# Second MLP: half of block 0's first product by seven products of quarters, temporaries and tables in pools of their stages

## The chip, the cores and the metric

One core of a Trainium2 chip runs the program in one launch. The metric is the device time of one execution in microseconds (us), the median of several runs. One core has five engines that run side by side, each through a queue of its own in order: TensorE (PE, matrix products; the loads of its stationary operand are shown apart as PEld), VectorE (DVE), ScalarE (ACT), GpSimd (POOL) and SyncE (SP, which here only issues DMA transfers).

## The reference, cut to what matters

Two layers work on 640 tokens (512 latent, 128 context) of width 1024. Layer 0 mixes tokens by pooling, layer 1 by retention, and each is followed by the MLP in question:

```python
def sq_relu_mlp(h, w1, w2):
    return jnp.square(jax.nn.relu(h @ w1)) @ w2

# per layer i, with shift, scale and gate from the conditioning vector
h = rmsnorm(x, norm_mlp_w[i]) * (1 + sc_m) + sh_m
x = x + g_m * sq_relu_mlp(h, mlp_w1[i], mlp_w2[i])      # w1 1024 x 4096, w2 4096 x 1024
```

The change lies in the MLP of layer 1 (the second MLP) and in where temporaries and small tables are kept.

## The kernel before

**Layout and precision.** Activations are held transposed: 8 tiles of 128 channels by 640 tokens, and the tokens go in two halves of 320 (`HALVES`). Every operand of a product is split into a high and a low part (`split`, L142: ScalarE casts the high part at L144, VectorE subtracts the low one at L145), and one product of tiles is three matmuls (`mm3`, L205 to L207). A plain product of one 128-column tile of the weights with one half of the tokens (`gemm`, L209) is 8 x 3 = 24 matmuls of 320 columns.

**The MLP.** `mlp` (L748 on) goes through four blocks of 1024 hidden channels. In each block the first product fills `act` (8 tiles n, two halves h): ScalarE's relu (L851) and square (L852), then a split. The second product adds to x (`add_to_x`, L500). Block 0 makes its first product plainly: `follow` (L530) makes tiles 0 to 3 while the norm of the second half of the tokens is still being computed, then tiles 4 to 7 come one by one. Blocks 1 to 3 (`FAST`) make theirs in two halves of four tiles, each by seven products of quarters in place of eight (`fast`, L812).

**Seven products of quarters.** `seven` (L790) loads two pieces of the weights (1 MB each), makes four sums of 128x1024 on VectorE (L802 to L806) and seven split operands. `quarters` (L767) makes the operands of the other side from the eight normed tiles `hm`: for each of four q it joins four high and low parts (L776), makes four sums (L777, L779, L781, L783) and splits them, three of them into a tile `both` of their own, shown as `tq` in the trace, and one over `hm[q]`'s second half in place. That is 12 operations of VectorE and 4 casts of ScalarE for each q, once for the MLP, ahead of block 1. Of the seven products, the first two read `hm[0..3]` and `hm[4..7]` of the first half as they are, the third and fourth read `tq`, the fifth what was written in place, the sixth `hm[4..7]` of the second half, the seventh `tq`. Each is 24 matmuls, with q as the inner index: of a product's two tiles of output, each takes q = 0, 1, 2, 3 in turn.

**What sets the order.** The Tile framework puts the program's instructions into the engines' queues ahead of time and places semaphores; the queues of the kernel before are not in the order of the text. For instance, the operations of `quarters` stand in the text behind block 0's whole second product, and in VectorE's queue among its `add_to_x`. Buffers are handed out per pool and tag: staged weights from `wst` (2 buffers), split weights from `wsp` (tags whi, wlo, 4 buffers each), temporaries by `th` and `t5` from `tmp` (tag t, 7 buffers of 128x512, for all stages of the kernel).

**Tables.** Retention's rotation table is the rear part of `tab_sb`, loaded at L644 on SP's queue near the start; its position tables `npos` and `ipos` (GpSimd, L734 to L737) and the constant `ones_v` (L232) are made when the engines come to them, and all stay in the pool `const` for the whole kernel.

Of the kernel before, what the change touches and what calls it, by code (L numbers as in the profile page):

```python
# [27 lines left out]
DV = 512  # L28
# [35 lines left out]

STEPS = (((0, 0, 0, 0, 3, 2, 3, 0), (0, 1, 0, 1, 0, 0, 0, 0)),
# [45 lines left out]
def hybrid_kernel(ctx: ExitStack, tc: tile.TileContext, x_prompt, x_sample, state_ret, c, c_ctx, w_ada, b_ada,  # L111
# [15 lines left out]
    tmp = ctx.enter_context(tc.tile_pool(name="tmp", bufs=1))  # L127
    psum = ctx.enter_context(tc.tile_pool(name="psum", bufs=8, space=PSUM))


    def bank():
        return psum.tile([128, 512], F32, tag="ps", name=nm("ps"))

# [4 lines left out]
    def t5():  # L138

        return tmp.tile([128, 512], F32, tag="t", name=nm("t"), bufs=7)  # L140
# [68 lines left out]
    def gemm(ws, act, h, mid=None):  # L209


        out = [bank()[:, 0:HALF] for _ in ws]
        for k in range(len(act)):
            if mid and k == len(act) // 2:
                mid()
            for o, w in zip(out, ws):
                mm3(o, [z[:, k] for z in w], [z[:, HALVES[h]] for z in act[k]], k == 0, k == len(act) - 1)
        return out
# [199 lines left out]
    xall = xp.tile([128, KD, TOK], F32, name="xall")  # L418
# [132 lines left out]
    with tc.tile_pool(name="pool", bufs=1) as pp:  # L551
        extra[:] = [(wst, 2), (pp, 3), (pp, 3), (wst, 2), (pp, 3)]
# [153 lines left out]
    def decays():  # L706
# [38 lines left out]
        tables.extend((lg, nlg, npos, ipos, zeta))  # L745
# [3 lines left out]
    def mlp(i, sq, norm, hm, step, along):  # L749

        with tc.tile_pool(name=f"hid{i}", bufs=1) as hid:

# [92 lines left out]

            for b in range(4):
                act = [[hid.tile([128, TOK], F32R, tag=f"a{n}{e}", name=nm("a")) for e in "hl"] for n in range(8)]

                def hidden(n, h, ps):
                    r, f = th(), th()  # L850
                    S.activation(r, ps, AF.Relu)  # L851
                    S.activation(f, r, AF.Square)  # L852
                    split(f, *[z[:, HALVES[h]] for z in act[n]])
# [9 lines left out]
                if b in FAST[i]:  # L863
                    if b == FAST[i][0]:
                        ops = quarters()
                    for half in range(2):
                        fast(b, half, ops, hidden)
                        if i == 0 and b == 3:
                            next(logs, None)
                            next(logs, None)  # L870
                    get(2 * b + 1, 0)
                else:
                    for n in range(4 if b == 0 else 0, 8):
                        if n == FREE:
                            room[0] = room[1]
                        for h in range(2):
                            hidden(n, h, gemm([get(2 * b, n)], hm, h)[0])
                        step(STEPS[b][0][n])
                if i == 0 and b == 0:
                    step(until=(0, 5))  # L880
                if b == 3:
                    room[:] = [None, None]
                    return tail(lambda n, h: gemm([get(7, n)], act, h)[0], mod[i][5], along)
                for n in range(KD):
# [22 lines left out]
    with tc.tile_pool(name="ret", bufs=1) as rp:  # L907
        def r5():
            return rp.tile([128, 512], F32R, tag="r5", name=nm("r5"), bufs=6)

        lg, nlg, npos, ipos, zeta = tables
# [5 lines left out]
        def queries_keys(hd):  # L917
# [10 lines left out]
            def take(nmq, t, h, ps):  # L928
                ct = C_ROPE if nmq == "q" else C_ROPE + 144
# [11 lines left out]
                if t == 0:  # L941
                    cb, sb = (tab_sb[:, ct + o:ct + o + 8][:, rw].unsqueeze(2).to_broadcast(shape) for o in (0, 8))
                else:
                    cb, sb = (tab_sb[:, ct + o:ct + o + 64].unsqueeze(1).to_broadcast(shape) for o in (16, 80))
# [301 lines left out]
```

## Time and profile before

| | |
|---|---|
| time, median of 3 runs | 1621.87 us (1620.45 to 1624.13) |
| the profiled execution's own time | 1622.77 us |
| its span, first to last instruction | 1621.0 us |
| mean granted clock of TensorE, share of full speed | 0.994 |
| matmuls | 9897 |

A row of a timeline gives the start from the span's begin, the duration, the engine, the line of the kernel, the operation, the tiles as output <- inputs, sizes, and in brackets the idle time of the engine before it and what ended that. Matmuls are pipelined: the distance of two starts is the pace, not the duration shown.

### The profile page before, as it was taken

The numbers are of one execution on the slowest core, as the hardware profiler recorded it, in microseconds if no ns is written. First come the engines' busy times: TensorE is split into PE (matmuls) and PEld (weight loads), VectorE is DVE, ScalarE is ACT, GpSimd is POOL, SyncE is SP. The second block draws the span as 40 slices with busy tenths as digits, with TensorE's granted clock in tenths as the row PEclk, the third lists the DMA queues.
The fourth block names the chain that finished last, engine by engine and source line by source line (L and its number), as shares of the span: only waits on it lengthen the run. The fifth ranks groups of instructions, "written<-read, shape, count | busy, mean of one in ns | idle before, by whom it ended". The sixth has DMA issues, their size and how long they took to land. (4 is left out here: it accounts for less than half of the span.)

```text
span 1621.0 us, 24493 instructions
## 1 busy us (share of the span) xinstructions
PE 1582.8 (98%) x9897; PEld 1473.6 (91%) x9897; DVE 1164.0 (72%) x2254; ACT 727.0 (45%) x1338; POOL 11.7 (1%) x26
## 2 busy tenths in 40 slices
PE   6999999999999999999999999999999999999997
PEld 3459999999999988889889988998899999999997
DVE  6879996676766687886797678778967573554654
ACT  6747326336156354433442443353464371451640
POOL 0000000000000000000000000000000000000000
PEclk9999999999999999999999999999999999999999
DMA  9744333333314123323304241322032132131221
GB/s 356 252 141 146 105 105 104 104 124 111 105 53 156 45 70 128 96 79 130 128 29 156 63 146 64 118 92 91 26 105 79 34 124 78 53 104 53 95 75 66
DMA packets 137954, 169.83 MB, mean 105 GB/s; under 512 B 3512, under 2 KB 111472, under 8 KB 137840
## 3 DMA queue, kind: packets, MB, share of 16 engines
q1 hardware_dynamic: 134800, 161.28, 30.2%
q0 software_dynamic: 1312, 4.20, 0.8%
q10 hardware_dynamic: 1728, 2.78, 0.5%
q8 instruction: 78, 1.28, 0.3%
q14 instruction: 36, 0.29, 0.1%
HBM read 161.43 MB, written 6.82 MB: 104 GB/s over the span
## 5 line engine op out<-in xcount | busy, mean ns | idle before, releaser
L144 ACT CAST whi<-wst 128x1024 fp32r<-128x1024 f32 x245 | 254.4, 1049 | 422.5 <-PE ps L206 200.8
L145 DVE TENSOR_TENSOR wlo<-wst,whi 128x1024 fp32r<-128x1024 f32 x245 | 297.3, 1223 | 136.5 <-ACT whi L144 124.0
L205 PE MATMUL ps<-a,whi 128*128 128x320 f32 x896 | 277.2, 310 | 1.2 <-ACT a L144 1.2
L206 PE MATMUL ps<-a,whi 128*128 128x320 f32 x896 | 277.3, 310 | 0.1
L207 PE MATMUL ps<-a,wlo 128*128 128x320 f32 x896 | 276.2, 309 | 0.0
L500 DVE SCALAR_TENSOR_TENSOR xall<-ps,mod,xall 128x320 f32<-128x320 f32 (+2 forms) x288 | 115.7, 436 | 151.6 <-PE ps L207 150.4
L206 PEld LDWEIGHTS ps<-a,whi 128*128 128x128 f32 x896 | 168.2, 188 | 2.1 <-DVE a L145 1.7
L205 PEld LDWEIGHTS ps<-a,whi 128*128 128x128 f32 x896 | 167.9, 188 | 1.8 <-ACT a L144 1.7
L207 PEld LDWEIGHTS ps<-a,wlo 128*128 128x128 f32 x896 | 168.0, 188 | 0.0
L389 DVE SCALAR_TENSOR_TENSOR acc<-wst,c,acc 128x256 f32<-128x256 f32 x336 | 137.6, 483 | 0.0
L205 PE MATMUL ps<-tq,whi 128*128 128x320 f32 x288 | 89.0, 309 | 0.0
L206 PE MATMUL ps<-tq,whi 128*128 128x320 f32 x288 | 89.0, 309 | 0.0
L207 PE MATMUL ps<-tq,wlo 128*128 128x320 f32 x288 | 89.0, 309 | 0.0
L206 PE MATMUL ps<-A,whi 128*128 128x320 f32 x256 | 78.9, 309 | 0.0
L205 PE MATMUL ps<-A,whi 128*128 128x320 f32 x256 | 78.9, 312 | 0.0
L207 PE MATMUL ps<-A,wlo 128*128 128x320 f32 x256 | 78.2, 309 | 0.0
L145 DVE TENSOR_TENSOR a<-t,a 128x320 fp32r<-128x320 f32 x128 | 61.8, 488 | 22.7 <-ACT a L144 22.2
L435 ACT ACTIVATE t<-xall 128x320 f32<-128x320 f32 x56 | 26.0, 471 | 81.2 <-DVE xall L500 81.2
L852 ACT ACTIVATE t<-t 128x320 f32<-128x320 f32 x128 | 60.5, 473 | 1.8
L144 ACT CAST a<-t 128x320 fp32r<-128x320 f32 x128 | 58.5, 457 | 1.5
L207 PEld LDWEIGHTS ps<-tq,wlo 128*128 128x128 f32 x288 | 54.1, 188 | 0.0
L205 PEld LDWEIGHTS ps<-tq,whi 128*128 128x128 f32 x288 | 54.1, 188 | 0.0
(406 smaller groups left out, 4004.4 us busy)
## 6 DMA issues: line engine op xcount, KB each, us to landing
wst<-in_mlp_w_dram SPq DMA_DIRECT2D x64, 1024.0 KB, 5.3
wst<-in_w_ada_dram SPq DMA_DIRECT2D x46, 1024.0 KB, 6.0
wst<-in_ret_w_in_dram SPq DMA_DIRECT2D x24, 1024.0 KB, 5.2
wst<-in_ret_w_out_dram SPq DMA_DIRECT2D x8, 1024.0 KB, 5.0
t<-in_state_ret_dram SPq DMA_DIRECT2D x16, 256.0 KB, 5.5
out_dram<-t POOLq DMA_DIRECT2D x16, 256.0 KB, 2.9
xt<-in_x_sample_dram SPq DMA_DIRECT2D x4, 512.0 KB, 4.8
both<-in_w_ada_dram SPq DMA_DIRECT2D x2, 1024.0 KB, 7.3
```

What stands on the lines that cost most here:

```text
L144: S.copy(hi, src)
L145: sub.tensor_tensor(lo, src, hi.bitcast(F32), ALU.subtract)
L205: T.matmul(out, wh, ah, start=first, stop=False, skip_group_check=more)
L206: T.matmul(out, wh, al, start=False, stop=False, skip_group_check=more)
L207: T.matmul(out, wl, ah, start=False, stop=last, skip_group_check=more)
L389: V.scalar_tensor_tensor(acc[j], w[:, k], by, acc[j], ALU.mult, ALU.add)
L435: S.activation(sq[:, o:o + t.shape[-1]], t, AF.Square)
L500: V.scalar_tensor_tensor(x, ps[:, cols], gate[:, d, j:j + 1], x, ALU.mult, ALU.add)
L852: S.activation(f, r, AF.Square)
```

## The change

In the second MLP (`PART = (False, True)`) block 0's second half, tiles 4 to 7, is made by `fast` in place of eight plain products. `quarters` is therefore called in block 0, right behind `follow`, and its result serves blocks 0 to 3. Temporaries come from the pool of the stage that is open (`pool`, `hid0`, `ret`, `hid1`), 7 buffers in each, in the MLPs 320 wide. The identity is a tile of its own; the rotation table, `npos`, `ipos` and `ones_v` are loaded or made at the start of the retention stage in its pool. A DRAM pool is opened in which no tile is made. The new functions `fast_to_x` and `hidden_quarters`, which would do the second product in the same way, are not called, since `BOTH` is empty for both MLPs; they are left out here.

```diff
+BOTH = ((), ())
+PART = (False, True)
...
+    stage = [None, 512]
...
     def t5():
-        return tmp.tile([128, 512], F32, tag="t", name=nm("t"), bufs=7)
+        return stage[0].tile([128, stage[1]], F32, tag="t", name=nm("t"), bufs=7)
...
-    tab_sb = const.tile([128, C_N], F32, name="tab_sb")
-    nc.scalar.dma_start(out=tab_sb[:, 0:C_ROPE], in_=tab[:, 0:C_ROPE])
-    ident = tab_sb[:, C_ID:C_ID + 128]
+    ident = const.tile([128, 128], F32, name="ident")
+    nc.scalar.dma_start(out=ident, in_=tab[:, C_ID:C_ID + 128])
...
-    ones_v = const.tile([128, 128], F32, name="ones_v")
-    V.memset(ones_v, 1.0 / DV)
...
     with tc.tile_pool(name="pool", bufs=1) as pp:
+        stage[:] = [pp, 512]
...
         def load_tables():
             nc.sync.dma_start(out=win_sb, in_=win)
-            nc.sync.dma_start(out=tab_sb[:, C_ROPE:], in_=tab[:, C_ROPE:])
...
-        npos = const.tile([128, 896], I16, name="npos")
-        G.iota(npos, [[1, 896]], base=-384, channel_multiplier=-1)
-        ipos = const.tile([128, 2, 512], I16, name="ipos")
-        G.iota(ipos[:, 0, :], [[1, 512]], base=1, channel_multiplier=0)
-        G.iota(ipos[:, 1, :], [[-1, 512]], base=512, channel_multiplier=0)
...
         with tc.tile_pool(name=f"hid{i}", bufs=1) as hid:
+            stage[:] = [hid, HALF]
...
             def get(b, n):
                 for o in range(1, AHEAD + 1):
-                    if b * 8 + n + o < 64 and not ((b * 8 + n + o) // 16 in FAST[i] and (b * 8 + n + o) // 8 % 2 == 0):
-                        gets[(b * 8 + n + o) // 8]((n + o) % 8)
+                    at = b * 8 + n + o
+                    if at < 64 and at // 16 not in (FAST, BOTH)[at // 8 % 2][i] and not (PART[i] and 4 <= at < 8):
+                        gets[at // 8](at % 8)
                 return gets[b](n)
...
-            def fast(b, half, ops, take):
-                col = b * 1024 + half * 512
-                ws = seven(mlp_w1[i, :, col:col + 512])
+            def fast(src, half, ops, take):
+                ws = seven(src[:, half * 512:(half + 1) * 512])
...
-                if b in FAST[i]:
-                    if b == FAST[i][0]:
+                if b in FAST[i] or b == 0 and PART[i]:
+                    if b == (0 if PART[i] else FAST[i][0]):
                         ops = quarters()
-                    for half in range(2):
-                        fast(b, half, ops, hidden)
+                    for half in range(b == 0, 2):
+                        fast(mlp_w1[i, :, blocks[b]], half, ops, hidden)
...
-                    get(2 * b + 1, 0)
+                    if b not in BOTH[i]:
+                        get(2 * b + 1, 0)
...
     with tc.tile_pool(name="ret", bufs=1) as rp:
+        stage[:] = [rp, 512]
...
+        npos = rp.tile([128, 896], I16, name="npos")
+        G.iota(npos, [[1, 896]], base=-384, channel_multiplier=-1)
+        ipos = rp.tile([128, 2, 512], I16, name="ipos")
+        G.iota(ipos[:, 0, :], [[1, 512]], base=1, channel_multiplier=0)
+        G.iota(ipos[:, 1, :], [[-1, 512]], base=512, channel_multiplier=0)
+        rope = rp.tile([128, C_N - C_ROPE], F32, name="rope")
+        nc.sync.dma_start(out=rope, in_=tab[:, C_ROPE:])
+        ones_v = rp.tile([128, 128], F32, name="ones_v")
+        V.memset(ones_v, 1.0 / DV)
```

## Rows read from the trace of the kernel before

**Rows 1.** The head of the page: span, then busy time, share of the span and instructions of each engine.

```profile
span 1621.0 us, 24493 instructions
PE 1582.8 (98%) x9897; PEld 1473.6 (91%) x9897; DVE 1164.0 (72%) x2254; ACT 727.0 (45%) x1338; POOL 11.7 (1%) x26
```

**Rows 2.** The waits of TensorE from 1150 us to the end: line, what it waited for, us in total, times, the longest.

```profile
PE ps L1188 <- DVE sqacc L447: 1.9, 1, 1.9
PE ps L205 <- DVE t L837: 1.4, 1, 1.4
```

**Rows 3.** The table by stretches: the stretch, its length, busy time and instructions of PE, PEld, DVE, ACT and POOL, the granted clock of TensorE, the DMA engines' share, GB/s. The five stretches are: the end of `follow`; block 0's tiles 4 to 7 and a little more; the `quarters` among block 0's second product; tiles 4 to 7 alone; a half of block 1 by seven products.

```profile
1193.00:1203.00 10.00, 10.00 (x70) 10.00 (x70) 5.67 (x10) 9.27 (x24) 0.00 (x0) 1.00 0.32 104
1203.00:1230.00 27.00, 27.00 (x186) 27.00 (x185) 10.35 (x15) 15.86 (x30) 0.00 (x0) 1.00 0.25 79
1230.00:1260.00 30.00, 30.00 (x207) 30.00 (x206) 29.66 (x66) 11.87 (x22) 0.00 (x0) 1.00 0.22 71
1200.30:1228.40 28.10, 28.10 (x194) 28.10 (x193) 11.37 (x16) 17.10 (x35) 0.00 (x0) 1.00 0.33 108
1284.80:1309.40 24.60, 24.60 (x168) 24.39 (x168) 15.59 (x21) 16.51 (x31) 0.00 (x0) 1.00 0.27 87
```

**Rows 4.** TensorE's timeline where block 0's tiles 4 to 7 begin and where they end and the second product begins.

```profile
1200.30 0.31 PE L205 MATMUL ps<-h0h,whi 128*128 128x320 f32 x1
...
1228.46 0.31 PE L205 MATMUL ps<-a,whi 128*128 128x320 f32 x1
```

**Rows 5.** TensorE's timeline in block 1, a half by seven products: the first matmuls of the first, second and third product, and of the next half's.

```profile
1284.78 0.31 PE L205 MATMUL ps<-h0h,whi 128*128 128x320 f32 x1
...
1288.30 0.31 PE L205 MATMUL ps<-h4h,whi 128*128 128x320 f32 x1
...
1291.82 0.31 PE L205 MATMUL ps<-tq,whi 128*128 128x320 f32 x1
...
1309.63 0.31 PE L205 MATMUL ps<-h0h,whi 128*128 128x320 f32 x1
```

**Rows 6.** VectorE's timeline of `quarters` in the second MLP: the first operations of q = 0, and the last low part of q = 3.

```profile
1230.74 0.48 DVE L776 TENSOR_TENSOR t<-h0h,h0l 128x320 f32<-128x320 f32 x1
1231.14 0.48 DVE L145 TENSOR_TENSOR a<-t,a 128x320 fp32r<-128x320 f32 x1
1231.55 0.49 DVE L776 TENSOR_TENSOR t<-h4h,h4l 128x320 f32<-128x320 f32 x1
...
1259.35 0.48 DVE L145 TENSOR_TENSOR tq<-t,tq 128x320 fp32r<-128x320 f32 x1
```

**Rows 7.** ScalarE's timeline of the last relu and square of tiles 0 to 3.

```profile
1201.75 0.43 ACT L851 ACTIVATE t<-ps 128x320 f32<-128x320 f32 x1
...
1202.42 0.49 ACT L852 ACTIVATE t<-t 128x320 f32<-128x320 f32 x1
```

**Rows 8.** VectorE's timeline in retention's first head. L1045 and L1048 both read only `npos` and a decay constant; L1045 writes a tile of a tag of its own, L1048 a temporary of tag t. L1012, in the text ahead of both, also writes a temporary of tag t.

```profile
577.14 0.70 DVE L1045 TENSOR_SCALAR dm<-npos,lg 128x896 f32<-128x896 int16 x1
...
629.42 0.48 DVE L1012 SCALAR_TENSOR_TENSOR t<-ps,zeta,t 128x256 fp32r<-128x256 f32 x1
629.81 0.81 DVE L1048 TENSOR_SCALAR t<-npos,lg 128x448 f32<-128x448 int16 x2
```

**Rows 9.** VectorE's groups by line and shape in the half by seven products of rows 3 (1284.8 to 1309.4): count, then busy time, mean ns of one, idle time before.

```profile
L145 DVE TENSOR_TENSOR wlo<-wst,whi 128x1024 fp32r<-128x1024 f32 x6 | 7.3, 1224 | 7.2 <-ACT whi L144 4.1 <-PE ps L207 3.1
L802 DVE TENSOR_TENSOR wst<-wst 128x1024 f32<-128x1024 f32 x1 | 1.2, 1224 | 0.1
```

**Rows 10.** TensorE's timeline in `follow`: the seventh tile's operand of the first pair is used before and after the second pair's first ones.

```profile
1174.30 0.94 PE L205 MATMUL ps<-h7h,whi 128*128 128x320 f32 x1
1175.03 0.47 PE L205 MATMUL ps<-h0h,whi 128*128 128x320 f32 x1
...
1179.18 0.31 PE L206 MATMUL ps<-h7l,whi 128*128 128x320 f32 x1
```

**Rows 11.** The table by stretches, columns as in rows 3, at the end of the waits in `follow`, and TensorE's timeline after the waits at the start of retention.

```profile
1173.00:1175.00 2.00, 1.77 (x5) 1.08 (x4) 2.00 (x5) 0.56 (x1) 0.00 (x0) 0.50 0.00 0
1175.00:1176.40 1.40, 1.40 (x7) 1.40 (x7) 1.40 (x3) 0.00 (x0) 0.00 (x0) 0.50 0.35 80
1176.40:1180.00 3.60, 3.60 (x26) 3.60 (x26) 3.46 (x7) 0.00 (x0) 0.00 (x0) 1.00 1.00 315
...
599.68 0.78 PE L992 MATMUL ps<-wlo,h0h 128*128 128x512 f32 x1
...
603.12 0.39 PE L992 MATMUL ps<-wlo,h0h 128*128 128x512 f32 x1
```

**Rows 12.** The timelines of SP and of POOL near the start.

```profile
7.83 0.43 SPq L644 DMA_DIRECT2D tab_sb<-in_tab_dram  x1
...
2.02 0.92 POOL L734 IOTA npos<- 128x896 int16 x1
2.86 0.59 POOL L736 IOTA ipos<- 128x512 int16 x1
```

**Rows 13.** The timelines of ScalarE and VectorE where the first MLP ends and retention begins: the decay powers from `ipos`, the first operation after ScalarE's pause, and the first use of the rotation table.

```profile
564.94 1.34 ACT L1042 ACTIVATE xi<-ipos,lg 128x512 f32<-128x512 int16 x2 [1.84 <-PE ps L207]
...
576.53 1.38 ACT L483 ACTIVATE t<-t,mod,a 128x192 f32<-128x192 f32 x3 [9.00 <-DVE t L481]
...
587.08 0.49 DVE L946 TENSOR_TENSOR q<-ps,tab_sb 128x320 f32<-128x320 f32 x1
```

More of the change, by code (lines that the diff above doesn't have):

```diff
@@ L216, in gemm @@
             for o, w in zip(out, ws):
-                mm3(o, [z[:, k] for z in w], [z[:, HALVES[h]] for z in act[k]], k == 0, k == len(act) - 1)
+                mm3(o, [z[:, k] for z in w], [z[h] if isinstance(z, list) else z[:, HALVES[h]] for z in act[k]], k == 0, k == len(act) - 1)
         return out
@@ L416, in scale_of @@
         return a
-    xall = xp.tile([128, KD, TOK], F32, name="xall")
+    xall = xp.tile([128, KD, TOK], F32, tag="xall", name="xall")
     xT = [xall[:, d, :] for d in range(KD)]
@@ L744, in decays @@
         S.activation(zeta, zeta, AF.Exp)
-        tables.extend((lg, nlg, npos, ipos, zeta))
+        tables.extend((lg, nlg, zeta))
     logs = decays()
@@ L844, in fast, with fast_to_x, put @@
                     w = after
-            for b in range(4):
[L847 to L853, printed above, removed]
+            def fast_to_x(src, half, ops):
+                ws = seven(src[:, half * 512:(half + 1) * 512])
+                banks = {}
+                def put(n, h, ps, gate):
+                    t = th()
+                    for j, cols in PARTS[h]:
+                        S.activation(t[:, cols], ps[:, cols], AF.Copy, scale=gate[:, n, j:j + 1])
+                    nc.gpsimd.dma_start(out=away[n][h], in_=t, accum_op=ALU.add)
+                w = next(ws)
+                for p, name in enumerate(("u", "c11", "u", "c21", "u", "u", "c21")):
+                    after = next(ws, None)
+                    for t in range(2):
+                        fresh = (name, t) not in banks
+                        if fresh:
+                            banks[name, t] = bank()[:, 0:HALF]
+                        ps = banks[name, t]
+                        for k in range(4):
+                            mm3(ps, [z[:, k, t * 128:t * 128 + 128] for z in w], ops[p][k], fresh and k == 0, k == 3, not fresh)
+                        n = half * 4 + t
+                        put(*((n, 0), (n, 0), (n + 2, 0), (n + 2, 1), (n + 2, 1), (n, 1), (n + 2, 0))[p], ps,
+                            minus if p in (2, 4) else mod[i][5])
+                    w = after
@@ new lines, in mlp, with hidden @@
+            spare = []
+            for b in range(4):
+                if b in BOTH[i]:
+                    hidden, places2 = hidden_quarters()
+                else:
+                    act = [[[hid.tile([128, HALF], F32R, tag=f"a{n}{h}{e}", name=nm("a")) for h in range(2)] for e in "hl"]
+                           for n in range(8)] if BOTH[i] else [
+                        [[z[:, HALVES[h]] for h in range(2)] for z in (hid.tile([128, TOK], F32R, tag=f"a{n}{e}",
+                                                                                name=nm("a")) for e in "hl")]
+                        for n in range(8)]
+                    def hidden(n, h, ps):
+                        r, f = th(), th()
+                        S.activation(r, ps, AF.Relu)
+                        S.activation(f, r, AF.Square)
+                        split(f, *[z[h] for z in act[n]])
@@ L862, in mlp @@
                     follow(sq, norm, [pair(0), pair(2)])
[L863 to L864 removed]
+                    if BOTH[i]:
+                        for n in range(KD):
+                            for h in range(2):
+                                nc.sync.dma_start(out=away[n][h], in_=xT[n][:, HALVES[h]])
+                if b in BOTH[i]:
+                    ops2 = places2()
+                if b in FAST[i] or b == 0 and PART[i]:
+                    if b == (0 if PART[i] else FAST[i][0]):
                         ops = quarters()
[L866 to L867 removed]
+                    for half in range(b == 0, 2):
+                        fast(mlp_w1[i, :, blocks[b]], half, ops, hidden)
                         if i == 0 and b == 3:
@@ L882, in mlp @@
                     room[:] = [None, None]
+                    if BOTH[i]:
+                        back = xp.tile([128, KD, TOK], F32, tag="xall", name="back")
+                        xT[:] = [back[:, d, :] for d in range(KD)]
+                        for n in range(KD):
+                            for h in range(2):
+                                nc.sync.dma_start(out=xT[n][:, HALVES[h]], in_=away[n][h])
                     return tail(lambda n, h: gemm([get(7, n)], act, h)[0], mod[i][5], along)
+                if b in BOTH[i]:
+                    for half in range(2):
+                        fast_to_x(mlp_w2[i, blocks[b]], half, ops2)
+                    continue
                 for n in range(KD):
```

66 lines of the change are left out of this document (62 added, 4 removed).

## Prediction

> **What bounds the kernel now.** I read the page's head first: TensorE is busy for 98% of a span of 1621.0 us, VectorE for 72%, ScalarE for 45% [rows 1]. Next TensorE's own waits from 1150 us on, where the second MLP lies: the two longest are 1.9 us at the very end and 1.4 us between two halves [rows 2]. So TensorE's stream sets the end there, and a matmul less is time won, but only if its operands come as early as they come now. The table by stretches shows what else runs: in block 0's tiles 4 to 7 TensorE has no idle time and VectorE is busy for 11.4 us of 28.1, yet where the quarters are made VectorE is busy for 29.7 us of 30 [rows 3]. The reader should see that the quarters are the heaviest piece of VectorE's work in this MLP and that today all of it lies beside the second product, which does not need it.
>
> **The matmuls removed.** Tiles 4 to 7 are now 4 x 2 x 24 = 192 matmuls, from 1200.30 to 1228.46 [rows 4]: 28.16 us, 0.1467 us each. Seven products are 168. In block 1 such a half runs from 1284.78 to 1309.63, 24.85 us, one product in 3.52 [rows 5]. With operands ready the change is worth 28.16 - 24.85 = 3.3 us.
>
> **The quarters moved.** Nothing is added to them; they are done once, as before, but their cover goes. Now they must stand between the end of `follow` and the third product. When can they start? Each needs temporaries of tag t, and these are handed out in the order of the text. Rows 8 show it: two operations with the same inputs, of which the one that writes a tile of its own ran at 577.14, and the one that writes a temporary only at 629.81, beside the temporary that precedes it in the text [rows 8]. Likewise the first joining operation of the quarters ran at 1230.74, beside the last low part of block 0's activations (1231.14), though its inputs were complete when `follow` ended at 1200.30 and VectorE had been idle for 16.7 us of the 27 from 1203 [rows 3, 4, 6]. In the changed kernel the temporaries ahead of them are those of the last relu and square of tiles 0 to 3, which end at 1202.42 + 0.49 = 1202.9 [rows 7]. A pool per stage keeps the 7 buffers and this order.
>
> How long do they take? 4 x 12 = 48 operations on VectorE, one each 0.41 us when they follow each other [rows 6]. The third and fourth product need q = 3 nearly last: all but two of the 48, so 46 x 0.41 = 18.9 us. Nothing else in between: ready at 1221.8. What can get in between are the weights' sums and low parts for products three to six: three sums and four low parts of 1.22 us [rows 9], 0 to 8.5 us. They come later in the text than the quarters and fill only places where VectorE waits for a cast, so I take 3.0, a third, nearer to the lower end: 1224.8. ScalarE's 16 casts (under 0.5 us each, some 8 us) hide behind VectorE's 18.9.
>
> What does TensorE do meanwhile? From 1200.30 the first two products run, 48 matmuls, until 1207.3. The weights for both can be split in time: tiles 0 and 1 free their buffers before `follow` ends. Then each q = 0, 1, 2 gives a few matmuls of the third product and, if the queue's order allows it, of the fourth. What is left when q = 3 is ready is 6 + 6 matmuls of these two and 72 of the last three: 84 x 0.1467 = 12.3 us. In the order of the text (the first tile's four q, then the second's) it is 111, so 16.3 us. That the framework does set products into each other is seen in `follow`, where the first pair's seventh operand is still used at 1179.18, after the second pair began at 1175.03 [rows 10]. I take 13.0. The second product of block 0 cannot fill the pause: its weights need the staging and split buffers that the seven products hold.
>
> **The clock after the pause.** After the waits in `follow` TensorE's granted clock was 0.50 (1.2 GHz) from 1173 to 1176.4 and 1.00 after that; after the waits at retention's start 8 matmuls took 3.44 us, from 599.68 to 603.12, where half of it is the loss at half speed [rows 11]. A pause of 14 us with a few matmuls in it is longer than either, so between 0 and 1.7 us is lost; I take 1.2. The Trainium skill ("TensorE: Matmul & The Clock Gate", section "Why this matters for your kernels") advises against gaps between bursts of matmuls because the clock goes back to half; that speaks against this change, and rows 11 agree with it (0.50). By that rule the sum has the whole 1.7, so 0.5 us more; if the trickle of matmuls kept the clock up, 1.2 less.
>
> **The tables and pools.** The table's load leaves the start: its issue took 0.43 us of SP's queue ahead of the first weights [rows 12], so between 0 and -0.4 us; I take -0.2, since the stage behind it waits in turn for VectorE. GpSimd's position tables (0.92 and 0.59 us) [rows 12] leave a queue that has nothing behind them. All of this comes to the start of retention, once the first MLP's buffers in that memory are free, about 567.5 (9.00 us of pause before 576.53). The decay powers (1.34 us) can no longer run at 564.94, but ScalarE's pause of 9.0 us covers them and the position tables; the rotation table is first read at 587.08, some 19 us later [rows 13]. Cost nothing, as long as SP's queue does not stand still (below). The temporaries' new places add waits on the memory of the stage before, whose last users are a few us earlier on the same engines: nothing either way.
>
> **The sum.** Operands 1224.8, + 13.0 + 1.2 = 1239.0 for the end of the first product, against 1228.46: +10.5; with -0.2 at the start +10.3. The profiled execution took 1622.77 us (span 1621.0 and 1.8 around it), 0.9 above the median of 1621.87. On its own scale that is 1633.1, on the median's 1632.2. Ends: 1221.8 + 12.3 = 1234.1 is +5.6, less 0.4 gives 1627.1; 1230.3 + 16.3 + 1.7 = 1248.3 is +19.8, so 1641.7.
>
> **The rivals.**
> (a) Not slower: the quarters get into VectorE's idle time inside `follow`. The place is 1193 to 1203, where VectorE is idle for 4.3 us [rows 3]. Used in full, the operands are ready at 1221.8 - 4.3 = 1217.5, the end is at 1229.8, +1.3 - 0.4, so 1622.8 with the weights' work wholly out of the way. It decides at 1228.46 - 12.3 = 1216.2: operands earlier than that make the change pay. Against it: the order of the temporaries [rows 6, 8]. For it: a fresh pool could let the order slip by one or two tiles.
> (b) Faster: the pause vanishes (operands by 1212.6, when TensorE has done all that q = 0 to 2 allow). Then -3.3 - 0.2: 1618.4. VectorE would have to have begun at 1193.7 and do nothing else, while it has 5.7 us of other work up to 1203 alone [rows 3].
> (c) Later still: SP's queue waits for the table's place with retention's weights behind it, from 564.9 to 567.5, and retention starts 2.6 us later: 1632.2 + 2.6 = 1634.8. Against it: the queue's order is made by when things are ready.
> (d) The change does not do what it says: the text leaves no doubt, 9897 matmuls [rows 1] become 9873.
>
> **How the numbers follow.** Forecast 0.83, (a) 0.06, (b) 0.05, (c) 0.06, which lies in the forecast's own range. Predicted 1632.2 us. The forecast's ends are 1627.1 and 1641.7; the two cases below hold 0.11, so they may stay out, and the range is 1626.5 to 1642. Slower by over 0.2% (3.2 us, about what a measurement here can tell from no change): forecast and (c), 0.89. Within 0.2%: (a) 0.06. Faster: (b) 0.05.
>
> **What would show it.** In the changed trace: the first joining operation of the quarters in the second MLP at about 1203, not before 1200; VectorE without idle time from there to about 1225; TensorE idle or in short bursts between 1207 and 1225, with waits on `tq` from VectorE or ScalarE, and a granted clock of 0.50 for part of it; block 0's first product ending about 1239 where it ended at 1228; VectorE far from full in block 0's second product, with no gain in TensorE's pace there; all else within 1 us. If the third product starts with no wait, the step on the temporaries' order is wrong. If the pause is there and the time is not, something at the tables or pools gave it back.

## The result and the profile after

The changed kernel takes 1642.77 us (median of 4 runs, 1642.23 to 1643.95) against 1621.16 of the kernel before on the same chip: ratio 1.0131, 95% interval 1.0114 to 1.0149, so 21.6 us slower. Forecast were 1632.2, and 1626.5 to 1642. The direction was right, and so was the main place, block 0 of the second MLP. The size was half, and a second place, retention's start, had been put at nothing.

The head of the page after (before: [rows 1]): 24 matmuls fewer, the span 19.5 us longer, TensorE's share 97% in place of 98%. The two profiled executions took 1622.77 and 1642.23 us, so they lie closer together than the medians.

```profile
span 1640.5 us, 24467 instructions
PE 1585.3 (97%) x9873; PEld 1475.0 (90%) x9873; DVE 1175.7 (72%) x2267; ACT 730.3 (45%) x1347; POOL 11.9 (1%) x26
```

TensorE's waits after, from 1190 us to the end (line, what it waited for, us in total, times, the longest). "issue" is a wait for which the profile shows no releaser.

```profile
PE ps L212 <- issue: 13.5, 1, 13.5
PE ps L1320 <- DVE sqacc L451: 1.9, 1, 1.9
PE ps L212 <- ACT whi L151: 1.8, 1, 1.8
PE ps L214 <- DVE wlo L152: 1.3, 1, 1.3
```

Before, there were two such waits, 1.9 and 1.4 [rows 2]; the 1.9 at the very end is still there, the 1.4 between two halves is gone. Three new ones stand in block 0's half by seven products ("the half" below). TensorE's timeline after, at their places: the half begins at 1201.95, four matmuls into the second product it stops, and the second product of the block begins at 1248.35.

```profile
1201.95 0.31 PE L212 MATMUL ps<-h0h,whi 128*128 128x320 f32 x1
...
1205.91 0.31 PE L213 MATMUL ps<-h4l,whi 128*128 128x320 f32 x1
1219.70 0.61 PE L212 MATMUL ps<-tq,whi 128*128 128x320 f32 x1 [13.47 <-issue]
...
1222.38 0.64 PE L214 MATMUL ps<-h4h,wlo 128*128 128x320 f32 x1 [1.28 <-DVE wlo L152]
...
1232.25 0.41 PE L212 MATMUL ps<-tq,whi 128*128 128x320 f32 x1 [1.80 <-ACT whi L151]
...
1248.35 0.31 PE L212 MATMUL ps<-a,whi 128*128 128x320 f32 x1
```

The half is 46.40 us long, where tiles 4 to 7 took 28.16 before [rows 4]: +18.2. At full clock its 168 matmuls are 24.65; the three gaps in the rows (13.79, 1.75 and 2.11 from start to start, the second from 1220.63; less 0.147 each) are 17.2; the other 4.55 are half clock. The table by stretches after shows where (columns as in [rows 3]):

```profile
1205.50:1219.70 14.20, 0.73 (x6) 0.49 (x5) 14.20 (x36) 6.22 (x15) 0.00 (x0) 0.65 0.00 1
1219.70:1222.40 2.70, 1.42 (x5) 1.02 (x5) 2.70 (x6) 0.68 (x2) 0.00 (x0) 0.50 0.00 0
1222.40:1226.80 4.40, 4.40 (x17) 4.40 (x18) 3.96 (x8) 1.68 (x5) 0.00 (x0) 0.51 0.00 0
1226.80:1232.20 5.40, 3.65 (x25) 3.39 (x24) 3.96 (x6) 4.06 (x10) 0.00 (x0) 1.00 0.00 0
...
1233.90:1237.00 3.10, 3.10 (x13) 3.10 (x13) 2.96 (x3) 1.56 (x3) 0.00 (x0) 0.51 0.05 14
```

VectorE is full from 1205.5 to 1219.7 while TensorE has 0.73 us of work; the clock is at half (1.2 GHz) behind the long pause, and at half once more behind the pause of 2.1 us. VectorE's timeline after tells what stands in its queue:

```profile
1202.26 1.22 DVE L803 TENSOR_TENSOR wst<-wst,wst 128x1024 f32<-128x1024 f32 x1
1203.39 0.48 DVE L776 TENSOR_TENSOR t<-h0h,h0l 128x320 f32<-128x320 f32 x1
...
1221.11 1.21 DVE L152 TENSOR_TENSOR wlo<-wst,whi 128x1024 fp32r<-128x1024 f32 x1
1222.25 0.48 DVE L152 TENSOR_TENSOR tq<-t,tq 128x320 fp32r<-128x320 f32 x1
...
1223.05 1.21 DVE L152 TENSOR_TENSOR wlo<-wst,whi 128x1024 fp32r<-128x1024 f32 x1
...
1226.26 0.48 DVE L152 TENSOR_TENSOR tq<-t,tq 128x320 fp32r<-128x320 f32 x1
...
1228.36 1.22 DVE L805 TENSOR_TENSOR wst<-wst 128x1024 f32<-128x1024 f32 x1
...
1229.90 1.22 DVE L806 TENSOR_TENSOR wst<-wst,wst 128x1024 f32<-128x1024 f32 x1
```

The row at 1221.11 is the low part of the **second** product's weights. Nothing in it depends on the quarters, yet it stands behind almost all of them, so 20 of the second product's 24 matmuls ran after the pause and not in it. The sums for the fourth product (1228.36 and 1229.90) stand behind all of them: that is the second pause. ScalarE's timeline after has the high part that this low part needs, done at 1203.1, and a copy that the next paragraph needs:

```profile
1202.05 1.04 ACT L151 CAST whi<-wst 128x1024 fp32r<-128x1024 f32 x1
...
1219.18 0.75 ACT L831 COPY t<-ps 128x320 f32<-128x320 f32 x2
```

The wait without a releaser, up to 1219.70, has one in the run with the part alone (e2 below), where it is as long:

```profile
PE ps L206 <- ACT t L833: 13.4, 1, 13.4
```

L833 there is ScalarE's copy of the first product's bank, onto which the third product adds; after, the copy ran at 1219.18, behind the quarters' casts in ScalarE's queue. It costs little by itself, because the low part of 1221.11 is later still.

A second place, which the forecast had put at nothing, is retention's start. Waits of TensorE from 560 to 630 us after; the wait of 2.5 us for a low part of the values' weights is new:

```profile
PE ps L1124 <- DVE wlo L152: 2.5, 1, 2.5
PE ps L1137 <- ACT whi L151: 1.4, 1, 1.4
```

The kernel before has in their place:

```profile
PE ps L1005 <- ACT pr L938: 2.1, 2, 1.4
```

Matched one by one with those of the kernel before, the matmuls fall back by 3.2 us between 564 and 620 us.

### The profile page after: what moved, and what is told of

The parts are those of the page before. It is cut to its first block, busy times and chain, and to the rows that moved or that the text cites. A ratio compares the mean times of both kernels' runs of the same rounds, so it can differ in the third digit from the quotient of the medians.

```text
span 1640.5 us, 24467 instructions
## 1 busy us (share of the span) xinstructions
PE 1585.3 (97%) x9873; PEld 1475.0 (90%) x9873; DVE 1175.7 (72%) x2267; ACT 730.3 (45%) x1347; POOL 11.9 (1%) x26
## 4 chain that ended last, share of the span: by engine, by line
PE 79%; DVE 10%; ACT 5%; DMA 4%; issue 1%; ACTq 0%; DVEq 0%; SPq 0%; POOLq 0%
PE ps L212 22%; PE ps L213 22%; PE ps L214 22%; PE ps L287 3%; DMA wst<-in_mlp_w_dram 3%; PE ps L1124 2%; PE ps L1122 2%; PE ps L1123 2%; DVE wlo L152 2%; ACT whi L151 2%; DVE acc L393 1%; PE ps L635 1%; DMA wst<-in_ret_w_in_dram 1%; PE ps L469 1%; ACT t L487 0%
## 5 line engine op out<-in xcount | busy, mean ns | idle before, releaser
L212 PE MATMUL ps<-tq,whi 128*128 128x320 f32 x312 | 97.6, 313 | 15.3 <-issue 13.5
L213 PE MATMUL ps<-tq,whi 128*128 128x320 f32 x312 | 97.2, 312 | 0.0
L214 PE MATMUL ps<-tq,wlo 128*128 128x320 f32 x312 | 96.9, 312 | 0.0
L212 PEld LDWEIGHTS ps<-tq,whi 128*128 128x128 f32 x312 | 59.4, 190 | 15.8 <-issue 13.7
L152 DVE TENSOR_TENSOR a<-t,a 128x320 fp32r<-128x320 f32 x128 | 61.7, 487 | 15.8 <-ACT a L151 15.5
L213 PEld LDWEIGHTS ps<-tq,whi 128*128 128x128 f32 x312 | 59.4, 191 | 0.0
L214 PEld LDWEIGHTS ps<-tq,wlo 128*128 128x128 f32 x312 | 59.2, 190 | 0.0
```

What stands on the lines that cost most here:

```text
L152: sub.tensor_tensor(lo, src, hi.bitcast(F32), ALU.subtract)
L212: T.matmul(out, wh, ah, start=first, stop=False, skip_group_check=more)
L213: T.matmul(out, wh, al, start=False, stop=False, skip_group_check=more)
L214: T.matmul(out, wl, ah, start=False, stop=last, skip_group_check=more)
```

## The experiments

Theory at the start: all of the loss lies in block 0, because the quarters have no cover and the seven products' own weights stand behind them in VectorE's queue. Rival 1: pools and tables carry several us. Rival 2: the length of the quarters alone decides, whatever the order. Rival 3: the half clock is the main part of the miss. (The text ahead of e4 calls the length of the quarters rival 3; rival 2 in the text ahead of e3 is that the products' own weights can't keep up.) Ratios are to the kernel before, in runs on the same chip.

The versions of the changed kernel in e4, e6, e7 and e10 differ from it by 1.5 to 4 us in time, and their intervals overlap with its own. What their edits do is therefore read from the traces too: the table has how much longer block 0 is than in the kernel before, from the last matmul of `follow` to the first of block 1.

| | us against before |
|---|---|
| changed kernel; e2, part alone | +18.4; +18.5 |
| e3, ready operands | -2.9 |
| e4, weights first | +15.1 |
| e6, joins on GpSimd; e9, no joins | +20.7; +9.7 |
| e7, filled pauses | +16.9 |
| e10, own temporaries | +15.8 |
| cover: e8; e11; e12; e15; e16 | +3.6; +7.2; +3.1; -1.2; -1.1 |

**Pools alone, part alone.** The changed kernel with the seven products in block 0 switched off, and the kernel before with nothing but these:

```
e1:  -PART = (False, True)
     +PART = (False, False)
e2:  kernel before, with PART, its branch in the loop over blocks and in get()
```

> The pools, the moved tables and the new code paths, without the seven products in block 0 of the second MLP. Theory (all of the loss is in block 0): 1621.2 + 0.95 (shift of the changed kernel's matmuls just before the second MLP) = 1622 us, within 0.2% of the kernel before. Rival 1 (pools and tables carry several us; retention's matmuls start 3.1 us later in the changed kernel): 1624 to 1627 us.

> The kernel before with the seven products in block 0 of the second MLP and nothing else: one pool of temporaries and the tables at the start, as before. Theory: nearly the whole loss, +19 to +21 us, so 1640 to 1642. Rival 1: +16 to +18, because the 3 us at retention's start are gone.

Measured: 1626.18, ratio 1.0024 (1.0013 to 1.0034), and 1638.98, ratio 1.0103 (1.009 to 1.0117). By the ratios pools and tables cost 3.9 us, the part 16.7; together 20.6, where the changed kernel's ratio gives 21.2. Rival 1 is right, and the theory as it was put (all in block 0) falls.

**Ready operands.** Seven products without quarters:

```
-    ops = quarters()
+    ops = [hm's own parts, seven times]    # block 0; quarters() ahead of block 1
```

> The changed kernel, but block 0's seven products take the normalized input's own parts as all seven operands, so they need no quarters (the numbers of tiles 4 to 7 of that block are not the reference's); the quarters are made ahead of block 1, as in the kernel before. Theory (seven products gain 3.3 us where their operands are ready; the quarters' place costs all of the loss): 3.3 us less than the run with the pools alone, so about 1618.7. Rival 2 (the seven products' own weights, sums and splits can't keep up here): 1622 or more even with operands ready.

Measured: 1621.75, ratio 0.9999 (0.999 to 1.0008), 4.4 us below the run with the pools alone (4.1 by the ratios). It is above the 1618.7 because that run, from which the theory counts, took 1626.18 in place of 1622. The half ran from 1202.50 to 1227.57, 25.07 us, with one wait in it:

```profile
PE ps L214 <- DVE wlo L152: 0.2, 1, 0.2
```

So the 24 matmuls are worth 3.1 us in the trace (forecast 3.3), the products' own weights keep up when no quarters are in VectorE's queue, and the rival that they can't is out.

**Weights first.** Four weight splits ahead of the quarters in the text:

```
+    ws = seven(mlp_w1[i, :, blocks[0]][:, 512:1024])
+    early = [next(ws) for _ in range(4)]
     ops = quarters()
```

> The changed kernel with the first four of block 0's seven weight splits (and the sums for them) ahead of the quarters in the text. VectorE's queue then has five more operations of 1.2 to 1.5 us ahead of or among the first quarters, and none of the next products' weights behind them. Theory (the miss of the forecast is the weights that stand behind the quarters): the second product runs inside the pause, the second pause (2.1 us) is gone; operands of q = 3 at about 1226 in place of 1222 to 1226, 13 us of matmuls behind them and 2 to 4 of half clock: block 0's first product ends at 1241 to 1244 in place of 1248.3, so 1636 to 1639 us. Rival 3 (the sheer length of the quarters decides, and the weights' work only moves): 1642 to 1646.

Measured: 1640.08, ratio 1.0108 (1.0094 to 1.0121), 2.7 us less than the changed kernel (3.7 by the ratios): between the theory's 1636 to 1639 and the rival's 1642 to 1646. In its trace the first two products run without a stop until 1209.9, and TensorE then waits for each q:

```profile
1214.25 0.60 PE L212 MATMUL ps<-tq,whi 128*128 128x320 f32 x2 [4.05 <-issue]
...
1218.93 0.90 PE L212 MATMUL ps<-tq,whi 128*128 128x320 f32 x2 [2.67 <-ACT tq L151]
...
1223.75 0.90 PE L212 MATMUL ps<-tq,whi 128*128 128x320 f32 x2 [2.67 <-ACT tq L151]
...
1235.19 0.42 PE L212 MATMUL ps<-h0h,whi 128*128 128x320 f32 x1 [1.74 <-ACT t L831]
```

The half takes 42.85 us in place of 46.40. The order is worth 3.5 us; the rest is the length of VectorE's chain, as rival 2 said.

**Shorter chains.** Once with the 16 joining operations on GpSimd, once without them:

```
e6:  -V.tensor_tensor(f, hi, lo, ALU.add)
     +(G if i == 1 else V).tensor_tensor(f, hi, lo, ALU.add)
e9:  the four joins of each q left out; subtract and add read the high parts
```

> The changed kernel with the 16 joining operations of the second MLP's quarters on GpSimd, which has no work there, in place of VectorE. VectorE's chain from about 1203 is 32 x 0.41 + 1.2 (the second product's low part, which now stands ahead of it) = 14.4 us if GpSimd keeps up. Theory (VectorE's queue sets both pauses): operands of q = 3 at about 1219 in place of 1222 to 1226, the weights behind them 4 to 5 us earlier, block 0's first product ends at about 1243 in place of 1248.3: 1637 to 1639 us. Rival (the half clock after the pause and the products left over set the end): less than 2 us, 1641 to 1643.

> The changed kernel with the 16 joining operations of the second MLP's quarters left out (the quarters are made of the high parts alone, so the numbers of blocks 0 to 3 there are coarser than the reference's). VectorE's chain from 1203 is 32 operations of 0.41 us, 13.1 in place of 19.7. Theory (one chain on VectorE, quarters first and the next products' weights behind them, sets both pauses): everything behind it comes 5.5 to 6.6 us earlier, 1636 to 1637.5 us. Rival (the length of the quarters is not what the end hangs on, but the products left over and the half clock): less than 3 us, 1640 to 1642.

Measured: e6 1646.16, ratio 1.0151 (1.0137 to 1.0164), above both its theory and its rival; its half is 48.71 us long, 2.3 more than the changed kernel's. e9 1633.88, ratio 1.0074 (1.0058 to 1.009), 8.9 us less than the changed kernel, more than forecast. Without joins the second product's low part came at 1203.77 instead of 1221.11, so its matmuls were back in the pause, and the long wait was 8.1 us: a shorter chain and a better order, both at once. On GpSimd the joins did not shorten the chain: the low part of q = 3 for the third product ended at 1230.62, after at 1226.74. GpSimd's timeline in e6:

```profile
1213.92 0.97 POOL L776 TENSOR_TENSOR t<-h5h,h5l 128x320 f32<-128x320 f32 x1 [0.90 <-DVE t L781]
1214.86 1.10 POOL L776 TENSOR_TENSOR t<-h2h,h2l 128x320 f32<-128x320 f32 x1
1216.39 1.04 POOL L776 TENSOR_TENSOR t<-h6h,h6l 128x320 f32<-128x320 f32 x1 [0.43 <-DVE tq L152]
```

VectorE's timeline in the same run:

```profile
1213.70 0.48 DVE L152 TENSOR_TENSOR h0l<-t,h0h 128x320 fp32r<-128x320 f32 x1
1214.10 1.14 DVE L783 TENSOR_TENSOR t<-t,t 128x320 f32<-128x320 f32 x1
1215.17 1.14 DVE L152 TENSOR_TENSOR tq<-t,tq 128x320 fp32r<-128x320 f32 x1
1216.23 0.48 DVE L777 TENSOR_TENSOR t<-t,t 128x320 f32<-128x320 f32 x1
```

The 16 joins take 0.9 to 1.9 us each there (spans on GpSimd are rough in the profile), and VectorE's operations of 0.48 us that start while one runs, as those at 1214.10 and 1215.17, take 1.14.

**The clock.** Matmuls that nobody reads fill the pauses:

```
+FILL = {1: 84, 3: 14}
...
+                    if PART[i] and p in FILL and p not in filled:
...
+                        idle = bank()[:, 0:HALF]      # a bank that nobody reads
+                        for o in range(FILL[p]):
+                            T.matmul(idle, ...)       # 320 columns
```

> The changed kernel with 84 matmuls of 320 columns that nobody reads ahead of the second product (12.3 us, 5 of them earlier) and 14 behind the third product (2.05 us), so that TensorE works through its two pauses and the clock need not fall; nothing else waits for them. Half clock costs 4.6 us between 1219.7 and 1237 in the changed kernel (46.4 us for the half, less 17.2 of pauses, less 24.65 at full clock). Theory (VectorE's queue sets the start of the fourth product at 1232.25, so clock won ahead of it only lengthens the second pause): 1.5 to 2.5 us less, 1640 to 1641. Rival (the clock is the main part of the miss): 4 to 5 us less, 1638 to 1639.

Measured: 1641.08, ratio 1.0122 (1.0108 to 1.0136), 1.7 us less; the half, 44.67 us, is shorter by as much. The table by stretches: the clock stays up through the filled pause, and the chain on VectorE sets the next start anyway (a wait of 1.9 us for the second product's low part, up to 1224.55). Behind that wait the clock is at half once more.

```profile
1206.00:1218.00 12.00, 12.00 (x84) 12.00 (x83) 12.00 (x31) 5.31 (x11) 0.00 (x0) 1.00 0.00 0
...
1224.00:1228.00 4.00, 3.45 (x14) 3.45 (x15) 3.62 (x7) 0.92 (x2) 0.00 (x0) 0.57 0.00 0
1228.00:1234.00 6.00, 6.00 (x43) 5.98 (x42) 5.08 (x10) 4.89 (x11) 0.00 (x0) 1.00 0.00 0
```

Rival 3 is out: of 4.55 us at half clock 1.7 come back, some 1.4 are still lost between 1224 and 1228 (14 matmuls in 3.45 us), and the rest falls into waits for VectorE.

**The start of the quarters.** Four temporaries of their own:

```
-    b11, b12, b21, b22 = (th() for _ in range(4))
+    b11, b12, b21, b22 = (hid.tile([128, HALF], F32, tag="b", name=nm("b"), bufs=4) if i else th()
+                          for _ in range(4))
```

> The changed kernel with four temporaries of their own for the second MLP's quarters, in place of those of tag t. Theory (the order in which the temporaries are handed out holds the quarters until the last activation of tiles 0 to 3): the first joining operation runs at about 1194 in place of 1203.4, in the 4.3 us that VectorE is idle from 1193 to 1203; the whole chain ends up to 4.3 us earlier, less what it delays in the normalization's last steps and the first product's weights (0 to 2 us): 1639 to 1641 us. Rival (the quarters' inputs, or VectorE's queue, would have kept them until 1203 anyway): no change, 1642 to 1643.5.

Measured: 1640.59, ratio 1.0115 (1.01 to 1.013), 2.2 us less. The first joining operation:

```profile
1188.38 0.48 DVE L777 TENSOR_TENSOR b<-h0h,h0l 128x320 f32<-128x320 f32 x1
```

15 us earlier than in the changed kernel, so it was the order of the temporaries that had held it. Most of the gain is lost again: the first product's weights now stand behind q = 0's casts in ScalarE's queue, and TensorE waits 4.2 us for them, up to 1206.4.

**Retention's start.** The changed kernel's tables and pools, without the seven products, and the table of ones back at the start; then one half of the edits each (no seven products):

```
e5:   +ones_v = const.tile([128, 128], F32)     # at the start; not in retention's pool
e13:  pools per stage, all tables at the start
e14:  one pool of temporaries, rotation and position tables in retention's pool, ones at the start
```

> The run with the pools alone (no seven products in block 0), but the table of ones of retention's norm (a tile of 128 x 128, set by one short operation on VectorE) is again made at the start of the kernel; the rotation table, the position tables and the pools stay as in the changed kernel. Theory (this one operation at retention's start shifts the queue's order on VectorE, so that the first low part of the values' weights stands behind other work, 600.43 in place of 598.28): the 2.7 us wait of the values' first products is gone, 3.5 to 4 us less than the run with the pools alone, so about 1622. Rival (the rotation table's load holds SP's queue, or the memory of the stage before is free too late): no change, 1625 to 1627.

> The kernel before with the temporaries in a pool per stage and nothing else of weight: all tables at the start as before, no seven products in block 0. Theory (the order at retention's start is the only cost of the second part of the change): no difference, 1620.5 to 1622.5 us. Rival (the pools' places in memory make waits of their own): 1623 to 1625, as the run with the ones back (1623.7).

> The kernel before with one pool of temporaries as before and the rotation and position tables in retention's memory, the table of ones at the start; no seven products in block 0. Theory: no difference, 1620.5 to 1622.5 us. Rival (the rotation table's load at retention's start, between the loads of weights on SP's queue, or the position tables, cost about 2 us): 1623 to 1625.

Measured: e5 1623.67, ratio 1.0014 (1.0005 to 1.0023); e13 1624.76, ratio 1.0016 (1.0007 to 1.0025); e14 1620.92, ratio 0.9992 (0.9984 to 1.0001). VectorE's timeline after, the table of ones and the values' first low part:

```profile
566.39 0.17 DVE L1043 MEMSET ones_v<- 128x128 f32 x1
...
600.43 1.22 DVE L152 TENSOR_TENSOR wlo<-wst,whi 128x1024 fp32r<-128x1024 f32 x1
```

The same low part before, and then in e5 with the ones back:

```profile
598.28 1.22 DVE L145 TENSOR_TENSOR wlo<-wst,whi 128x1024 fp32r<-128x1024 f32 x1
```

```profile
598.20 1.22 DVE L152 TENSOR_TENSOR wlo<-wst,whi 128x1024 fp32r<-128x1024 f32 x1
```

TensorE's longest wait from 560 to 630 us with the ones back, one that the kernel before has too:

```profile
PE ps L1137 <- ACT pr L1070: 2.2, 2, 1.5
```

In the trace the theory holds: the wait for the low part is gone. And not in this pair alone: the wait, 2.3 to 2.7 us, is in all eight traces whose table of ones is made in retention (after, e1, e3, e4, e6, e7, e9, e10), and in none of the ten where it is made at the start. Between 564 and 620 us the eight lose 2.9 to 4.2 us against the kernel before, the others between -1.7 and +1.7; e5 gains 1.0, because the clock behind the waits that it shares with the kernel before was at 1.00 where that kernel's was at half (rows in the last section). In time only 1.6 us from e1 to e5 show, with some 2 of uncertainty.

The moved tables cost nothing (e14). The pools alone cost 2.6 us (1.1 to 4.1), which the rival foresaw. The runs of e13 lie between 1621.5 and 1628.8 us, and the profiled one took 1622.6, below their median, so the trace doesn't show where these 2.6 us are. This stays open.

**Cover.** If the loss is missing cover, the change should pay under one. Block 0's second product is split by its K: tiles 0 to 3 first, beside the quarters, then the seven products, then the rest. It adds 24 gated sums into the residual on VectorE.

```
+    second(0)             # rows 0 to 511 of the block's w2, 192 matmuls
+    ops = quarters()
+    fast(0, 1, ops, hidden)
+    second(1)
```

e8: joins on GpSimd. e11: joins on VectorE, two weight splits ahead of the quarters. e12: the same on the changed pools, own temporaries, ones at the start. e15: the third and fourth split ahead of q = 2 and q = 3. e16: the fifth too.

> The kernel before, with the seven products in block 0 of the second MLP under cover: the second product of block 0 is split by its K of 1024 into two halves; the first half (tiles 0 to 3, 192 matmuls, 28.2 us) runs right behind them and hides the quarters, then the seven products, then the second half. Adds 24 gated sums into the residual on VectorE (0.4 us each); the joins are on GpSimd; tables and temporaries as before. Theory (the loss is that the quarters had no cover): the 3.3 us of the 24 matmuls come out, 1617.5 to 1619. Rival (VectorE, with 13.2 us of quarters, 9.6 of sums and some 10 of weights in 35 us, sets the end again, or the joins are slow on GpSimd): 1621 to 1626.

> The kernel before with the seven products in block 0 under the first half of the second product's K, as in the run under cover, but all joins on VectorE, and the first two of the seven weight splits ahead of the quarters in the text. In the run under cover the only long wait was 3.3 us for the first product's low part, behind the quarters in VectorE's queue, and VectorE's operations were up to 2.4 times as long beside GpSimd's. Theory: both are gone, and what is left is VectorE's own load of some 39 us in 35.6: 1619 to 1621 us. Rival (VectorE stays the bound, the wait only moves to the third product): 1622 to 1625.

> The same cover with the first two weight splits ahead of the quarters, on the changed kernel's pools, with the quarters' temporaries of their own (they fit in the memory that the shorter temporaries leave) and the table of ones made at the start again. The quarters' first eight operations move into VectorE's idle time inside follow. Theory: VectorE has some 4 us less to do under the cover, no wait is left, the 3.3 us of the 24 matmuls come out: 1617.5 to 1619.5 us. Rival (the first quarters delay the normalization's own steps inside follow, or the pools cost their own 2 us as in the run with the ones back): 1620 to 1623.

> The cover with its own temporaries, and the third and fourth weight splits placed between the quarters in the text (ahead of q = 2 and of q = 3). In the run before it (1623.95) the one long wait, 3.3 us at 1240, was for the fourth product's weights: their last sum ran at 1237.3, behind all quarters, though its inputs were there by 1230. Theory: that wait goes, the quarters of q = 3 end 2.4 us later and the third product waits 1 to 2 us for them, the half clock behind it is shorter: 1.5 to 3 us less, 1621 to 1622.5. Rival (VectorE has too much to do under the cover, so any order waits as long): 1623.5 to 1625.

> The cover with its own temporaries as in the run before it (1620.77), and the fifth weight split too ahead of the quarters of q = 3 in the text. There the one wait left in block 0 was 2.2 us, ahead of the fifth product, for its low part, which stood behind the last quarters in VectorE's queue. Theory (the place of the weights in VectorE's queue): the wait goes, and the quarters of q = 3 end 1.2 us later, just in time or up to 1 us late: 1 to 2 us less, 1618.5 to 1620, below the kernel before. Rival (VectorE has as much to do as there is time, so the wait moves to the third or sixth product): 1620.5 to 1622.

Measured: e8 1623.75, ratio 1.0016 (1.0006 to 1.0025); e11 1628.51, 1.0037 (1.0025 to 1.0049); e12 1623.95, 1.0011 (1.0002 to 1.0019); e15 1620.77, 0.9996 (0.9988 to 1.0005); e16 1622.23, 0.9998 (0.9989 to 1.0007). In e8 the rival was right: VectorE stays the bound. e11 came out above even its rival's range. In e12 the theory (no wait is left) fell, and its rival named neither the time nor the wait, which is for weights whose sum stands behind the quarters on VectorE. TensorE's longest wait in block 0 in e12:

```profile
PE ps L212 <- ACT whi L151: 3.0, 1, 3.0
```

In e15:

```profile
PE ps L212 <- ACT t L836: 1.9, 1, 1.9
```

In e16:

```profile
PE ps L212 <- ACT t L836: 1.3, 1, 1.3
```

From e12 to e15 only the place of two weight splits changed: the wait for the weights went, and 2.4 us came off by the ratios, as the theory said (4.3 in the table of block 0). The expectation of e16 had the wrong cause: L836 there is ScalarE's copy of a bank onto which the fifth product adds, behind casts in ScalarE's queue, and not the low part; the wait became shorter and did not go. With cover and order the loss is gone: in the traces of e15 and e16 block 0 is 1.2 and 1.1 us shorter than before, less than the 3.3 of the 24 matmuls by about the waits that are left. In time no version was measurably faster than the kernel before.

## Why the prediction came out half

The step that failed is the one on what TensorE does meanwhile: the second product was to run in the pause, and did not (120 matmuls, 17.6 us, were left where 13.0 us were taken). A second step, the tables and pools put at nothing, failed beside it.

**Matmuls: right.** -3.3 forecast, -3.1 in the trace with ready operands.

**Start of the quarters: right, and its reason shown.** 1203 forecast, 1203.39 measured, though in a stream of matmuls that was 1.65 us later there (1201.95 against 1200.30); with temporaries of their own 1188.38.

**Length of the chain: right within 2 us.** q = 3 was ready for the third product at 1226.74, forecast 1224.8, a start later by 0.4 included.

**"The weights for both can be split in time" and the 13.0 us left over: wrong, and the largest miss.** The text takes 84 to 111 matmuls as left when q = 3 is ready, because the first two products and q = 0 to 2 lie in the pause. There were 120, 17.6 us: the second product's low part stood behind the quarters on VectorE, and in TensorE's queue q = 1 to 3 of the third product stood behind the rest of the second. With the splits ahead (e4) both products ran in the pause.

**Weights' work of 3.0 us as a delay of the operands: not the whole of it.** 2.4 us of it came between the quarters; the sums and splits for the fourth product came behind them and made a pause of their own, 1.96 us net, for which the sum has no term. The sentence that the weights' work would "fill only places where VectorE waits for a cast" failed: VectorE had no such places from 1205.5 to 1219.7.

**Clock: mis-sized.** 1.2 us taken (0 to 1.7). Behind q = 3 it was 2.0: 1226.74 + 17.6 + 1.96 + 2.0 = 1248.3. Another 2.5 went before, on the second product, where they count as part of the wait. Against 1239.0 forecast the end is 9.35 later: 1.9 from the operands, 4.6 from the matmuls left over, 2.0 from the second pause, 0.8 from the clock. That the upper end of the forecast's sum is 1248.3 too is chance: there it is 1230.3 + 16.3 + 1.7.

**Tables and pools, -0.2: wrong.** +3.9 us in time (2.1 to 5.5), and 3.2 in the changed trace at retention's start. Rival (c) had that place and nearly the size, 2.6, but the wrong mechanism: with the rotation table loaded there (e14) nothing is lost, and with the table of ones made there the wait for a low part on VectorE is in every trace. The step looked for waits on memory and on DMAs, and passed over the table of ones, one operation of 0.17 us: moved, it changes the order that the planner writes for work behind it. In time 1.6 us go with it; the 2.6 us of the pools alone (e13) were put at nothing as well, and their cause stays open.

**"All else within 1 us": not quite.** The wait of 1.4 us between two halves [rows 2] is gone in the changed kernel, 1.1 us to its good.

Rivals (a), (b) and (d) did not come. (a) was worth trying, since with own temporaries the quarters do start inside `follow`; but there they delay the first product's weights.

## What to carry to other kernels

When an operand-making step is moved ahead of its first use, list not only its own length but everything that the planner puts behind it in the same queue, above all work that does not depend on it: here a low part of 1.2 us behind 19 us of quarters cost 20 matmuls their place in the pause. Cover is counted on the engine that makes the operands, not on the one that waits: 28 us of matmuls beside the quarters cut block 0's loss from 18.4 us to between 3 and 7, and removed it only after VectorE's order was also put right. A small operation moved to another place in the text can reorder a queue far from the edit; compare the order of the queues, not only the costs of what moved.

## What was not expected of the hardware

VectorE's operations on two inputs in SBUF of 128x320 took 1.14 us instead of 0.48 when they started while GpSimd ran a join, and the join itself took 0.9 to 1.9 us: 16 joins moved to an otherwise idle engine made the half 2.3 us longer. The Trainium skill ("GPSIMD Engine Reference", section "1. Specifications") says that GpSimd's access to SBUF is shared with VectorE and that they contend when VectorE's instruction has two inputs in SBUF; the rows agree, with a factor of 2.4.

TensorE's granted clock was at half (0.50 and 0.51) behind the pause of 13.8 us and once more behind the one of 2.1 us, though between the two it had been at 1.00 for some 3.4 us of matmuls. Keeping TensorE busy through the pause gave back 1.7 of 4.55 us.

At retention's start the kernel before and e5 have the same waits, 2.1 and 2.2 us in two pieces, and yet not the same clock behind them. The table by stretches before, then in e5:

```profile
599.60:602.60 3.00, 3.00 (x8) 2.43 (x9) 3.00 (x9) 0.70 (x2) 0.00 (x0) 0.50 0.00 0
```

```profile
599.60:602.60 3.00, 3.00 (x14) 2.47 (x14) 3.00 (x9) 0.70 (x2) 0.00 (x0) 1.00 0.00 0
```

The same eight matmuls took 3.45 us in the one and 1.93 in the other, so 1.5 us of a comparison of two traces can be the clock and not the edit.
